# Batched 8 KB casting loads, interleaved transposes, two-bank evacuations and one store queue in a Q·Kᵀ kernel

## Chip, cores and metric

The kernel runs on one core of a Trainium2 chip. The metric is the device time of one execution in microseconds (us). Most figures are medians of several executions. In every run that lists both, the time is about 1.8 us above the span of the profile (for example 1071.39 and 1069.6 us for one execution of the changed kernel).

## The reference

```python
batch, n_heads, seq, head_dim = 8, 12, 1024, 64      # q, k: float32, 96 heads
np.einsum('bhid,bhjd->bhij', q, k).astype(np.float32)  # out: 8 x 12 x 1024 x 1024 float32
```

The kernel reads 50.3 MB and writes 402.7 MB. The product itself is small, so this is a kernel about moving bytes.

## The kernel before

For each head, two DMAs on the GpSimd queue load Q and K and cast them from float32 to float16. Partition p gets rows 8p to 8p+7 of the head. That is one run of 2 KB in memory, written as 1 KB. PE transposes both (K twice, for the upper and the lower 64 partitions), DVE copies the transposes to SBUF, PE makes 16 products of 128x512, and DVE and ACT evacuate each PSUM bank. (PE writes its products to PSUM; a bank here is a tile of 128x512 float32, and to evacuate it is to copy it to SBUF, from where it is stored.) One store of 4 MB per head goes out, on the SP queue for even heads and on the ACT queue for odd ones.

```python
    in_pool = ctx.enter_context(tc.tile_pool(name="in_pool", bufs=24))
    out_pool = ctx.enter_context(tc.tile_pool(name="out_pool", bufs=5))
    ...
    for bh in range(BH):
        q_sb = in_pool.tile([P, NT, D], MM_DT, tag="in")
        k_sb = in_pool.tile([P, NT, D], MM_DT, tag="in")
        nc.gpsimd.dma_start(out=q_sb, in_=qf[bh].rearrange("(p t) d -> p t d", p=P))
        nc.gpsimd.dma_start(out=k_sb, in_=kf[bh].rearrange("(p t) d -> p t d", p=P))
        ...  # 4 transposes of Q, 16 of K; 2 copies by DVE
        for n in range(2):
            for t in range(NT):
                ps = po_pool.tile([P, 512], mybir.dt.float32, tag="po")
                nc.tensor.matmul(ps, ...)
                ...  # evacuated by DVE or ACT, one bank at a time
        out_eng = nc.sync if bh % 2 == 0 else nc.scalar
        out_eng.dma_start(out=of[bh].rearrange("(p t) j -> p (t j)", p=P), in_=o_sb)
```

Of the kernel before, what the change touches and what calls it, by code (L numbers as in the profile page):

```python
# [1 line left out]

# [5 lines left out]


MM_DT = mybir.dt.float16


@with_exitstack
def kernel(
    ctx: ExitStack,
    tc: tile.TileContext,
    q: bass.AP,
    k: bass.AP,
    out: bass.AP,  # L20
):
    nc = tc.nc

    B, H, S, D = q.shape
    P = 128
    NT = S // P
    assert D == 64 and S % P == 0 and NT == 8

    qf = q.rearrange("b h s d -> (b h) s d")
    kf = k.rearrange("b h s d -> (b h) s d")  # L30
    of = out.rearrange("b h i j -> (b h) i (j)")
    BH = B * H

    consts = ctx.enter_context(tc.tile_pool(name="consts", bufs=1))
    ident = consts.tile([P, P], MM_DT)
    make_identity(nc, ident)

    in_pool = ctx.enter_context(tc.tile_pool(name="in_pool", bufs=24))
    tr_pool = ctx.enter_context(tc.tile_pool(name="tr_pool", bufs=3))
    out_pool = ctx.enter_context(tc.tile_pool(name="out_pool", bufs=5))  # L40
    pt_pool = ctx.enter_context(tc.tile_pool(name="pt_pool", bufs=1, space=bass.MemoryType.PSUM))
    po_pool = ctx.enter_context(tc.tile_pool(name="po_pool", bufs=6, space=bass.MemoryType.PSUM))

    for bh in range(BH):
        q_sb = in_pool.tile([P, NT, D], MM_DT, tag="in")
        k_sb = in_pool.tile([P, NT, D], MM_DT, tag="in")
        nc.gpsimd.dma_start(out=q_sb, in_=qf[bh].rearrange("(p t) d -> p t d", p=P))  # L47
        nc.gpsimd.dma_start(out=k_sb, in_=kf[bh].rearrange("(p t) d -> p t d", p=P))  # L48

        t_ps = pt_pool.tile([P, 12, P], MM_DT, tag="pt")  # L50
        qT_ps = t_ps[:, 0:4]
        kT_ps = t_ps[:, 4:12]
        for e in range(4):
            nc.tensor.transpose(qT_ps[:, e], q_sb[:, 2 * e : 2 * e + 2], ident)  # L54
        for t in range(NT):
            nc.tensor.transpose(kT_ps[0:64, t], k_sb[:, t], ident)  # L56
            nc.tensor.transpose(kT_ps[64:128, t], k_sb[:, t], ident)  # L57

        qT_sb = tr_pool.tile([P, 4, P], MM_DT, tag="qT")
        kT_sb = tr_pool.tile([P, P, NT], MM_DT, tag="kT")  # L60
        nc.vector.tensor_copy(out=qT_sb, in_=qT_ps)  # L61
        nc.vector.tensor_copy(out=kT_sb, in_=kT_ps.transpose([0, 2, 1]))  # L62
        kT_j = kT_sb.rearrange("pp p t -> pp (p t)")

        o_sb = out_pool.tile([P, NT, S], mybir.dt.float32, tag="out")
        for n in range(2):
            for t in range(NT):
                h = (t % 2) * 64
                e = t // 2
                ps = po_pool.tile([P, 512], mybir.dt.float32, tag="po")  # L70
                nc.tensor.matmul(  # L71
                    ps,
                    qT_sb[h : h + 64, e],
                    kT_j[h : h + 64, n * 512 : (n + 1) * 512],
                )
                idx = n * NT + t
                if idx % 2 == 0 and idx < 14:
                    nc.vector.tensor_copy(  # L78
                        out=o_sb[:, t, n * 512 : (n + 1) * 512], in_=ps
                    )  # L80
                else:
                    nc.scalar.copy(  # L82
                        out=o_sb[:, t, n * 512 : (n + 1) * 512], in_=ps
                    )
        out_eng = nc.sync if bh % 2 == 0 else nc.scalar
        out_eng.dma_start(
            out=of[bh].rearrange("(p t) j -> p (t j)", p=P), in_=o_sb
        )


# [1 line left out]
_INS = ['q', 'k']  # L92
_OUTS = [((8, 12, 1024, 1024), 'float32')]


# [23 lines left out]
```

## Time and profile before

The time is 1075.96 us, the median of three executions (1073.93 to 1078.4). The profile has a span of 1077.5 us.

| | before |
|---|---|
| PE, DVE, ACT busy | 61%, 52%, 44% of the span |
| DMA engines | busy from start to end |
| a store packet (32 KB) | 1213 ns on ACT's queue, 1226 ns on SP's (medians of the packet records) |
| a load packet (2 KB read, 1 KB written) | 98 ns (median) |

The lines below are the DMA rows of the page's 40 slices and its queue table. In the queue table, q1 and q10 are the store queues of SP and ACT, q0 is the casting loads and q8 fetches PE's instructions. The last column is the time of the packets as a share of 16 engines' span.

```profile
DMA  9999999999999999999999999999999999999998
GB/s 230 391 426 420 428 415 386 422 355 421 422 385 392 422 425 360 421 423 397 367 422 426 347 421 423 386 396 364 421 417 391 393 422 421 353 419 423 353 425 373
...
q1 hardware_dynamic: 6912, 201.33, 43.8%
q10 hardware_dynamic: 6912, 201.33, 43.6%
q0 software_dynamic: 27648, 25.18, 14.5%
q8 instruction: 27, 0.44, 0.1%
```

Every digit of the DMA row is 9 but the last, so the engines are the limit. The GB/s row counts written bytes. A cast writes half of what it reads, so a slice full of loads looks slow in that row without being slow. Most dips to about 350 are such slices. The last one also holds a real gap: from 1012 to 1016 us the DMA share is 0.24.

From the view of waits (engine, line, what it waited for: us in total, times, longest):

```profile
PEld L56 <- DMA k_sb<-in_k_dram: 210.4, 31, 16.9
PE t_ps L56 <- DMA k_sb<-in_k_dram: 192.7, 23, 16.0
PE t_ps L54 <- DMA q_sb<-in_q_dram: 114.2, 15, 14.1
DVE o_sb L78 <- DMA out_dram<-o_sb: 7.1, 3, 3.6
ACT o_sb L82 <- DMA out_dram<-o_sb: 6.5, 3, 2.8
```

PE waits for loads. It hardly ever happens that an output buffer is still full. From the issue table, a load of 128 KB takes 34.7 to 39.5 us to land:

```profile
q_sb<-in_q_dram POOLq DMA_DIRECT2D x96, 128.0 KB, 39.5
k_sb<-in_k_dram POOLq DMA_DIRECT2D x96, 128.0 KB, 34.7
```

### The profile page before, as it was taken

Reading aid. Unit: us, or ns where it says so; the run is one execution under the profiler, and the core shown is the slowest. Engines: PE = TensorE matmul, PEld = TensorE weight load, DVE = VectorE, ACT = ScalarE, POOL = GpSimd, SP = SyncE. Lnnn points to the kernel's source line nnn. Section 1 sums busy time; section 2 is a strip of 40 time slices with the busy share of each in tenths; the row PEclk is TensorE's granted clock in tenths of the full one; section 3 lists DMA queues with packets and bytes.
Section 4 is the critical chain, followed back from the end, with each engine's and each line's share of the span. In section 5 each row is a group of like instructions: output and inputs, shape, how many; then the busy total and the mean of one; then the engine's idle time right before and its main releaser. Section 6 shows DMA issues by size and latency. Waiting matters only on the chain.

```text
span 1077.5 us, 9569 instructions
## 1 busy us (share of the span) xinstructions
PE 654.1 (61%) x3456; PEld 211.4 (20%) x3456; DVE 564.9 (52%) x864; ACT 469.5 (44%) x865; POOL 102.1 (9%) x198
## 2 busy tenths in 40 slices
PE   6888428458718627817693784665871862684470
PEld 2222102112202202202221221111220220221120
DVE  5686426447618625816473482544761862483360
ACT  4475315336506514615362462434650651463360
POOL 6100001020002002000200200102000100200000
PEclk9995555656556755855555565555655675565555
DMA  9999999999999999999999999999999999999998
GB/s 230 391 426 420 428 415 386 422 355 421 422 385 392 422 425 360 421 423 397 367 422 426 347 421 423 386 396 364 421 417 391 393 422 421 353 419 423 353 425 373
DMA packets 41519, 428.44 MB, mean 398 GB/s; under 512 B 4608, under 2 KB 29184, under 8 KB 29184
## 3 DMA queue, kind: packets, MB, share of 16 engines
q1 hardware_dynamic: 6912, 201.33, 43.8%
q10 hardware_dynamic: 6912, 201.33, 43.6%
q0 software_dynamic: 27648, 25.18, 14.5%
q8 instruction: 27, 0.44, 0.1%
q14 instruction: 20, 0.16, 0.0%
HBM read 50.33 MB, written 402.65 MB: 420 GB/s over the span
## 4 chain that ended last, share of the span: by engine, by line
PE 34%; another core or an unknown queue 25%; DMA 21%; DVE 15%; issue 2%; ACT 1%; POOL 0%; DVEq 0%; POOLq 0%; ACTq 0%
PE ps L71 21%; DMA q_sb<-in_q_dram 13%; DVE o_sb L78 7%; DVE kT_sb L62 6%; PE t_ps L56 5%; DMA k_sb<-in_k_dram 5%; PE t_ps L57 4%; PE t_ps L54 4%; DMA out_dram<-o_sb 3%; DVE qT_sb L61 1%; ACT o_sb L82 1%; POOL q_sb L47 0%; POOL k_sb L48 0%; DVEq L78 0%
## 5 line engine op out<-in xcount | busy, mean ns | idle before, releaser
L82 ACT COPY o_sb<-ps 128x512 f32<-128x512 f32 x864 | 468.2, 595 | 577.4 <-PE ps L71 564.9
L78 DVE COPY o_sb<-ps 128x512 f32<-128x512 f32 x672 | 427.3, 682 | 212.3 <-ACT o_sb L82 124.4
L71 PE MATMUL ps<-kT_sb,qT_sb 64*128 64x512 f16 x1536 | 485.7, 552 | 39.0 <-DVE o_sb L78 29.6
L56 PE MATMUL t_ps<-ident,k_sb 128*64 128x128 f16 x768 | 143.1, 303 | 192.7 <-DMA k_sb<-in_k_dram 192.7
L61 DVE COPY qT_sb<-t_ps 128x512 f16<-128x512 f16 x96 | 40.2, 418 | 269.4 <-PE ps L71 258.6
L54 PE MATMUL t_ps<-ident,q_sb 128*128 128x128 f16 x384 | 68.5, 280 | 160.5 <-DMA q_sb<-in_q_dram 114.2
L57 PE MATMUL t_ps<-ident,k_sb 128*64 128x128 f16 x768 | 151.5, 303 | 0.0
L71 PEld LDWEIGHTS <-qT_sb 64*128 64x128 f16 x1536 | 94.5, 105 | 195.1 <-issue 162.2
L56 PEld LDWEIGHTS <-k_sb 128*64 128x64 f16 x768 | 74.0, 144 | 250.6 <-DMA k_sb<-in_k_dram 210.4
L62 DVE COPY kT_sb<-t_ps 128x1024 f16<-128x1024 f16 x96 | 116.4, 1213 | 0.0
L57 PEld LDWEIGHTS <-k_sb 128*64 128x64 f16 x768 | 76.9, 143 | 107.7 <-issue 107.7
L47 POOL DMA_DIRECT2D q_sb<-in_q_dram x96 | 51.1, 532 | 423.9 <-PE ps L71 146.8
L48 POOL DMA_DIRECT2D k_sb<-in_k_dram x96 | 50.9, 530 | 423.7 <-PE t_ps L57 205.3
L54 PEld LDWEIGHTS <-q_sb 128*128 128x128 f16 x384 | 31.6, 113 | 280.7 <-issue 145.9
L82 ACT ACT_TABLE_LOAD x1 | 1.3, 1283 | 0.7 <-PEq L103 0.7
masks.py:199 POOL TENSOR_SCALAR_AFFINE_SELECT ident<-ident 128x128 f16<-128x128 f16 x1 | 0.3, 305 | 0.1
masks.py:197 POOL MEMSET ident<- 128x128 f16 x1 | 0.2, 204 | 0.3 <-POOLq L103 0.3
L103 POOL MEMSET const-float32-0.0<- 128x1 f32 x1 | 0.1, 98 | 0.2 <-issue 0.2
L103 POOL MEMSET const-bfloat16-1.0<- 128x1 bf16 x1 | 0.1, 101 | 0.0
L103 POOL MEMSET const-uint8-127<- 128x1 uint8 x1 | 0.1, 101 | 0.0
L103 POOL MEMSET const-float32-1.0<- 128x1 f32 x1 | 0.1, 98 | 0.0
## 6 DMA issues: line engine op xcount, KB each, us to landing
out_dram<-o_sb SPq DMA_DIRECT2D x48, 4096.0 KB, 25.6
out_dram<-o_sb ACTq DMA_DIRECT2D x48, 4096.0 KB, 26.8
q_sb<-in_q_dram POOLq DMA_DIRECT2D x96, 128.0 KB, 39.5
k_sb<-in_k_dram POOLq DMA_DIRECT2D x96, 128.0 KB, 34.7
```

The costliest lines, as they stand in the source:

```text
L47: nc.gpsimd.dma_start(out=q_sb, in_=qf[bh].rearrange("(p t) d -> p t d", p=P))
L48: nc.gpsimd.dma_start(out=k_sb, in_=kf[bh].rearrange("(p t) d -> p t d", p=P))
L54: nc.tensor.transpose(qT_ps[:, e], q_sb[:, 2 * e : 2 * e + 2], ident)
L56: nc.tensor.transpose(kT_ps[0:64, t], k_sb[:, t], ident)
L57: nc.tensor.transpose(kT_ps[64:128, t], k_sb[:, t], ident)
L61: nc.vector.tensor_copy(out=qT_sb, in_=qT_ps)
L62: nc.vector.tensor_copy(out=kT_sb, in_=kT_ps.transpose([0, 2, 1]))
L71: nc.tensor.matmul(ps, qT_sb[h : h + 64, e], kT_j[h : h + 64, n * 512 : (n + 1) * 512],)
L78: nc.vector.tensor_copy(out=o_sb[:, t, n * 512 : (n + 1) * 512], in_=ps)
L82: nc.scalar.copy(out=o_sb[:, t, n * 512 : (n + 1) * 512], in_=ps)
L103: nc = _bacc.Bacc("TRN2", target_bir_lowering=False, num_devices=1)
```

## The change

The intent is to make loads cheaper and earlier. Q and K of four heads are loaded by one DMA each, so that a partition gets a run of 8 KB. The next batch's transposes are placed between this batch's products, evacuations take two banks at once, and all stores go to the SP queue, which leaves ACT free.

Because partition p now holds 32 rows of a four-head block, DVE has to spread the transposed rows over the heads. It uses four small strided copies for Q instead of one.

The core of the diff:

```diff
-    in_pool = ... bufs=24          # one head each
-    out_pool = ... bufs=5
-    po_pool = ... bufs=6           # tiles of one bank
+    sizes = [1, 1, 2] + [GMAX] * (BH // GMAX - 1)     # GMAX = 4
+    in_pool = ... bufs=4           # a batch of up to four heads each
+    out_pool = ... bufs=4
+    po_pool = ... bufs=3           # tiles of two banks
...
+            for src, dst in ((qf, self.q_sb), (kf, self.k_sb)):
+                nc.gpsimd.dma_start(
+                    out=dst[:, : self.R],
+                    in_=src[rows].rearrange("(p r) d -> p r d", p=P),
+                )
...
+            for g in range(G):
+                ms = slice(g * pp, (g + 1) * pp)
+                nc.vector.tensor_copy(out=qT[:, g, :, :, a], in_=t_ps[:, 0:4, ms])
+            nc.vector.tensor_copy(out=kT[:, :, :, a], in_=t_ps[:, 4:12].rearrange("c t (g m) -> c g m t", g=G))
...
+                ps = po_pool.tile([P, S], F32, tag="po")
+                for n in range(2):
+                    nc.tensor.matmul(ps[:, n * 512 : (n + 1) * 512], ...)
+                if t in (1, 4, 6):
+                    nc.vector.tensor_copy(out=o_sb[:, t], in_=ps)
+                else:
+                    nc.scalar.copy(out=o_sb[:, t], in_=ps)
-        out_eng = nc.sync if bh % 2 == 0 else nc.scalar
-        out_eng.dma_start(...)
+            nc.sync.dma_start(...)
...
+    for i, b in enumerate(batches):
+        if i + AHEAD < len(batches):          # AHEAD = 3
+            batches[i + AHEAD].load()
+        for g in range(b.G):
+            b.scores(g)
+            ... nxt.transpose(a)              # the next batch's transposes
```

More of the change, by code (lines that the diff above doesn't have):

```diff
@@ L8 @@
 from concourse._compat import with_exitstack
-MM_DT = mybir.dt.float16
+F16 = mybir.dt.float16
+F32 = mybir.dt.float32
+P = 128
 @with_exitstack
@@ L24 @@
     B, H, S, D = q.shape
-    P = 128
     NT = S // P
-    assert D == 64 and S % P == 0 and NT == 8
-    qf = q.rearrange("b h s d -> (b h) s d")
-    kf = k.rearrange("b h s d -> (b h) s d")
-    of = out.rearrange("b h i j -> (b h) i (j)")
     BH = B * H
-    consts = ctx.enter_context(tc.tile_pool(name="consts", bufs=1))
-    ident = consts.tile([P, P], MM_DT)
-    make_identity(nc, ident)
-    in_pool = ctx.enter_context(tc.tile_pool(name="in_pool", bufs=24))
-    tr_pool = ctx.enter_context(tc.tile_pool(name="tr_pool", bufs=3))
@@ L40 @@
-    out_pool = ctx.enter_context(tc.tile_pool(name="out_pool", bufs=5))
-    pt_pool = ctx.enter_context(tc.tile_pool(name="pt_pool", bufs=1, space=bass.MemoryType.PSUM))
-    po_pool = ctx.enter_context(tc.tile_pool(name="po_pool", bufs=6, space=bass.MemoryType.PSUM))
-    for bh in range(BH):
-        q_sb = in_pool.tile([P, NT, D], MM_DT, tag="in")
-        k_sb = in_pool.tile([P, NT, D], MM_DT, tag="in")
-        nc.gpsimd.dma_start(out=q_sb, in_=qf[bh].rearrange("(p t) d -> p t d", p=P))
-        nc.gpsimd.dma_start(out=k_sb, in_=kf[bh].rearrange("(p t) d -> p t d", p=P))
-        t_ps = pt_pool.tile([P, 12, P], MM_DT, tag="pt")
-        qT_ps = t_ps[:, 0:4]
-        kT_ps = t_ps[:, 4:12]
-        for e in range(4):
-            nc.tensor.transpose(qT_ps[:, e], q_sb[:, 2 * e : 2 * e + 2], ident)
-        for t in range(NT):
-            nc.tensor.transpose(kT_ps[0:64, t], k_sb[:, t], ident)
-            nc.tensor.transpose(kT_ps[64:128, t], k_sb[:, t], ident)
-        qT_sb = tr_pool.tile([P, 4, P], MM_DT, tag="qT")
-        kT_sb = tr_pool.tile([P, P, NT], MM_DT, tag="kT")
-        nc.vector.tensor_copy(out=qT_sb, in_=qT_ps)
-        nc.vector.tensor_copy(out=kT_sb, in_=kT_ps.transpose([0, 2, 1]))
-        kT_j = kT_sb.rearrange("pp p t -> pp (p t)")
-        o_sb = out_pool.tile([P, NT, S], mybir.dt.float32, tag="out")
-        for n in range(2):
@@ new lines @@
+    GMAX = 4
+    assert D == 64 and NT == 8 and BH % GMAX == 0
+    qf = q.rearrange("b h s d -> (b h s) d")
+    kf = k.rearrange("b h s d -> (b h s) d")
+    of = out.rearrange("b h i j -> (b h) i j")
+    sizes = [1, 1, 2] + [GMAX] * (BH // GMAX - 1)
+    assert sum(sizes) == BH
+    consts = ctx.enter_context(tc.tile_pool(name="consts", bufs=1))
+    ident = consts.tile([P, P], F16)
+    in_pool = ctx.enter_context(tc.tile_pool(name="in_pool", bufs=4))
+    tr_pool = ctx.enter_context(tc.tile_pool(name="tr_pool", bufs=2))
@@ new lines, with __init__, load, alloc @@
+    out_pool = ctx.enter_context(tc.tile_pool(name="out_pool", bufs=4))
+    pt_pool = ctx.enter_context(
+        tc.tile_pool(name="pt_pool", bufs=1, space=bass.MemoryType.PSUM)
+    )
+    po_pool = ctx.enter_context(
+        tc.tile_pool(name="po_pool", bufs=3, space=bass.MemoryType.PSUM)
+    )
+    class Batch:
+        def __init__(self, first, G):
+            self.first, self.G, self.R = first, G, 8 * G
+        def load(self):
+            rows = slice(self.first * S, (self.first + self.G) * S)
+            self.q_sb = in_pool.tile([P, GMAX * NT, D], F16, tag="q")
+            self.k_sb = in_pool.tile([P, GMAX * NT, D], F16, tag="k")
+            for src, dst in ((qf, self.q_sb), (kf, self.k_sb)):
+                nc.gpsimd.dma_start(
+                    out=dst[:, : self.R],
+                    in_=src[rows].rearrange("(p r) d -> p r d", p=P),
+                )
+        def alloc(self):
+            self.qT = tr_pool.tile([P, GMAX * 4 * P], F16, tag="qT")
+            self.kT = tr_pool.tile([P, GMAX * S], F16, tag="kT")
+        def transpose(self, a):
+            G, pp = self.G, P // self.G
+            t_ps = pt_pool.tile([P, 12, P], F16, tag="pt")
+            for e in range(4):
+                r = a * NT + 2 * e
+                nc.tensor.transpose(t_ps[:, e], self.q_sb[:, r : r + 2], ident)
+            for t in range(NT):
+                rows = self.k_sb[:, a * NT + t]
+                nc.tensor.transpose(t_ps[0:64, 4 + t], rows, ident)
+                nc.tensor.transpose(t_ps[64:128, 4 + t], rows, ident)
+            qT = self.qT[:, : G * 4 * P].rearrange(
+                "c (g e m a) -> c g e m a", g=G, e=4, m=pp
+            )
+            kT = self.kT[:, : G * S].rearrange(
+                "c (g m a t) -> c g m a t", g=G, m=pp, t=NT
+            )
+            for g in range(G):
+                ms = slice(g * pp, (g + 1) * pp)
+                nc.vector.tensor_copy(out=qT[:, g, :, :, a], in_=t_ps[:, 0:4, ms])
+            nc.vector.tensor_copy(
+                out=kT[:, :, :, a],
+                in_=t_ps[:, 4:12].rearrange("c t (g m) -> c g m t", g=G),
+            )
+        def scores(self, g):
+            bh = self.first + g
+            qT = self.qT.rearrange("c (g e m) -> c g e m", e=4, m=P)
+            kT = self.kT.rearrange("c (g j) -> c g j", j=S)
+            o_sb = out_pool.tile([P, NT, S], F32, tag="out")
@@ L67 @@
             for t in range(NT):
                 h = (t % 2) * 64
-                e = t // 2
-                ps = po_pool.tile([P, 512], mybir.dt.float32, tag="po")
-                nc.tensor.matmul(
-                    ps,
-                    qT_sb[h : h + 64, e],
-                    kT_j[h : h + 64, n * 512 : (n + 1) * 512],
-                )
-                idx = n * NT + t
-                if idx % 2 == 0 and idx < 14:
-                    nc.vector.tensor_copy(
-                        out=o_sb[:, t, n * 512 : (n + 1) * 512], in_=ps
-                    )
-                else:
-                    nc.scalar.copy(
-                        out=o_sb[:, t, n * 512 : (n + 1) * 512], in_=ps
-                    )
@@ L85 @@
-        out_eng = nc.sync if bh % 2 == 0 else nc.scalar
-        out_eng.dma_start(
-            out=of[bh].rearrange("(p t) j -> p (t j)", p=P), in_=o_sb
-        )
+                ps = po_pool.tile([P, S], F32, tag="po")
+                for n in range(2):
+                    nc.tensor.matmul(
+                        ps[:, n * 512 : (n + 1) * 512],
+                        qT[h : h + 64, g, t // 2],
+                        kT[h : h + 64, g, n * 512 : (n + 1) * 512],
+                    )
@@ new lines, in scores @@
+                if t in (1, 4, 6):
+                    nc.vector.tensor_copy(out=o_sb[:, t], in_=ps)
+                else:
+                    nc.scalar.copy(out=o_sb[:, t], in_=ps)
+            nc.sync.dma_start(
+                out=of[bh].rearrange("(p t) j -> p (t j)", p=P),
+                in_=o_sb.rearrange("p t j -> p (t j)"),
+            )
+    batches, first = [], 0
+    for G in sizes:
+        batches.append(Batch(first, G))
+        first += G
+    AHEAD = 3
+    for b in batches[:AHEAD]:
+        b.load()
@@ new lines @@
+    make_identity(nc, ident)
+    batches[0].alloc()
+    for a in range(batches[0].G):
+        batches[0].transpose(a)
+    for i, b in enumerate(batches):
+        if i + AHEAD < len(batches):
+            batches[i + AHEAD].load()
+        nxt = batches[i + 1] if i + 1 < len(batches) else None
+        if nxt:
+            nxt.alloc()
+        for g in range(b.G):
+            b.scores(g)
+            if nxt:
+                for a in range(g * nxt.G // b.G, (g + 1) * nxt.G // b.G):
+                    nxt.transpose(a)
```

## The prediction

> **What bounds the kernel now.** The DMA engines, by bytes. The page's slices show them 90% busy or more from start to end; its queue table gives the store queues 43.8% + 43.6% and the load queue 14.5% of 16 engines' span, together 102% (packet records overlap a little). PE is busy 61%, DVE 52%, ACT 44%. A late stretch without loads (1040 to 1060 us) moves 423 to 432 GB/s. The Trainium skill ("DMA: Bandwidth & Descriptors", Where 436 GB/s comes from) puts the ceiling at 435 GB/s; this trace agrees within some 1 to 3%.
>
> In the packet records a store packet (32 KB) takes 1213 ns; a load packet (2 KB read, 1 KB written) 98 ns. In the pure-load stretch (9 to 18 us) the loads write 200 GB/s, so read 400 GB/s: about 82 ns a packet net of overlap, against 75 ns for 2 KB at the stores' rate. The 50.3 MB of reads already run at over 90% of line rate; that is why I expect little.
>
> Estimate from these numbers: 402.7 MB at 431 GB/s is 934 us; 24576 load packets at 82 ns on 16 engines, 126 us; 7 us of start and end; sum 1067. The other 10 us of the 1077.5 us span are holes and overhead. At 1011 to 1016 us the stores have run dry and PE waits 11 us for q_sb; some 3.7 us of DMA time is lost. Near 744 to 750 us about 1.2 us more.
>
> **Why the holes.** The queues take turns packet by packet (the skill, same page, Queues, rings and completion order). The trace agrees: from 60 to 140 us, loads read 0.26 MB per 20 us, one 2 KB packet for two 32 KB store packets. Loads starve (q_sb lands 39.5 us after issue) until the stores run dry. PE waits 307 us for q_sb and k_sb (waits view), mostly while DMA is busy.
>
> **What the change does.**
> - 8 KB load packets, a quarter as many: estimated 301 ns plus 8 to 20 fixed, in place of 4 x 82. Saves about 6 us (3 to 8).
> - One store queue, 8 KB per turn: loads get 1/5 of the bytes and need 1/9. Late holes close: about 5 us.
> - Two-bank evacuations, interleaved transposes, four strided qT copies in place of one: per head I estimate ACT 5 x 1.05 us, DVE 3 x 1.25 plus 2, PE 7. A store takes 9.7 us, with loads 11. All off the path.
> - One store queue for two: nothing; stretches with one or two move 430 to 432 GB/s alike.
> - Start: loads go out 0.7 us earlier, the identity 3 us later (after seven issues of 0.55 us); a wash. 4 output buffers suffice.
>
> Gain: about 11 us of DMA time, plus 2 to 3 us of smaller gaps.
>
> **Predicted: 1062 us, range 1055 to 1069. Faster by over 2%: 0.08; within 2%: 0.90; slower by over 2%: 0.02.**
>
> **What would show it.** Load packets 27648 to about 7500; share 14.5% to about 11.5%; stores still about 87%; no late dip. PE's waits on q_sb and k_sb shrink from 307 us to under 50; ACT and DVE wait for out_dram<-o_sb (13.6 us before) for hundreds of us: compute blocked by full output buffers. The chain becomes mostly stores.
>
> **What would make it wrong.** Faster than 1055: two store queues cost switching time that I don't see, or loads hide behind stores. Slower than 1069: an 8 KB cast packet costs over 330 ns; strided DVE copies, or PE stalled on the single transpose buffer, push compute beyond 11 us a head; an uneven share among the engines leaves tails.

## More of the kernel before

The kernels of one call ran on one chip together with the kernel before.

## The result

The changed kernel takes 1071.83 us (median of four executions, 1071.3 to 1072.35), against 1076.89 us for the kernel before beside it (four executions). The ratio is 0.9955, with a 95% interval of 0.9938 to 0.9972. Ratios here are the mean time of one kernel's runs over that of the other's of the same rounds, so they are not quite the ratio of the medians.

In e10 the changed kernel took 1070.61 us (ratio 0.9925, interval 0.9901 to 0.9949). The gain is about 5 to 7 us. 14 us had been predicted, and the time lies above the predicted range.

The same lines of the profile after (q0 are the loads, q1 all stores; there is no q10):

```profile
DMA  9999999999999999999999999999999999999996
GB/s 213 394 382 386 380 400 414 394 420 396 410 410 384 422 398 410 411 389 419 401 397 424 390 419 401 400 419 389 415 406 399 422 430 430 429 434 432 431 431 292
...
q1 hardware_dynamic: 13824, 402.66, 88.0%
q0 software_dynamic: 7488, 25.17, 11.9%
q8 instruction: 27, 0.44, 0.1%
```

The late dips are gone, and after the last load (837 us) the stores run at 422 to 434 GB/s. But the very last slice is down to 6 tenths and 292 GB/s. The waits:

```profile
ACT o_sb L114 <- DMA out_dram<-o_sb: 359.1, 87, 7.3
DVE o_sb L112 <- DMA out_dram<-o_sb: 213.8, 47, 7.5
PEld L78 <- DMA q_sb<-in_q_dram: 4.2, 1, 4.2
```

The mechanism turned round as it was meant to. PE waits 4.2 us for loads (before a weight load), and 573 us of ACT's and DVE's idle time is waiting for a free output buffer. From the chain that ended last, by engine, first before and then after:

```profile
PE 34%; another core or an unknown queue 25%; DMA 21%; DVE 15%; issue 2%; ACT 1%; POOL 0%; DVEq 0%; POOLq 0%; ACTq 0%
DMA 77%; PE 7%; ACT 7%; DVE 1%; issue 0%; ACTq 0%
```

So what is the last slice? The next lines give stretches of the end of both profiles. The columns are the stretch and its length in us, the busy time of each engine, PE's granted clock, the mean share of the 16 DMA engines that is busy, and GB/s. First the kernel before:

```profile
1060.00:1070.00 10.00, 0.00 (x0) 0.00 (x0) 0.00 (x0) 0.00 (x0) 0.00 (x0) 0.50 1.07 459
1070.00:1074.00 4.00, 0.00 (x0) 0.00 (x0) 0.00 (x0) 0.00 (x0) 0.00 (x0) 0.50 0.95 410
1074.00:1077.00 3.00, 0.00 (x0) 0.00 (x0) 0.00 (x0) 0.00 (x0) 0.00 (x0) 0.50 0.03 11
```

And the changed kernel:

```profile
1040.00:1050.00 10.00, 0.00 (x0) 0.00 (x0) 0.00 (x0) 0.00 (x0) 0.00 (x0) 0.50 1.02 439
1050.00:1058.00 8.00, 0.00 (x0) 0.00 (x0) 0.00 (x0) 0.00 (x0) 0.00 (x0) 0.50 0.98 422
1058.00:1062.00 4.00, 0.00 (x0) 0.00 (x0) 0.00 (x0) 0.00 (x0) 0.00 (x0) 0.50 0.57 246
1062.00:1066.00 4.00, 0.00 (x0) 0.00 (x0) 0.00 (x0) 0.00 (x0) 0.00 (x0) 0.50 0.19 82
1066.00:1069.00 3.00, 0.00 (x0) 0.00 (x0) 0.00 (x0) 0.00 (x0) 0.00 (x0) 0.50 0.03 11
```

In the kernel before, the DMA engines stop together. In the changed one they stop one after the other over 10 us: a share of 0.19 is three of sixteen engines. No compute engine has anything left to do.

A store raises its semaphore once for each of the 16 engines that finish their part of it, so the trace has 16 landing times for each store. They show how far apart the engines are. For the last store (my count from the semaphore records; us from the span's start):

| kernel | first | mean of 16 | second last | last | time (median) |
|---|---|---|---|---|---|
| before | 1074.9 | 1075.1 | 1075.6 | 1076.6 | 1076.9 |
| changed | 1058.4 | 1062.0 | 1067.0 | 1068.7 | 1071.8 |

The average engine gained 13.1 us, and the last one 7.9 us. The profile of e10, the changed kernel again, has the same tail: mean 1061.6, last 1067.9. In the changed kernel the distance between the first and the last landing (here called the lag) grows through the run:

```
store number     0    16    32    48    64    80    95
before          3.4   2.6   2.6   1.7   0.9   4.8   1.7   us
changed         1.4   4.7   6.1   7.2   7.6   8.6  10.3   us
```

### The profile page after: what moved, and what is told of

Its sections match the earlier page's. It is cut to its first block, busy times and chain, and to the rows that moved or that the text cites. A ratio compares the mean times of both kernels' runs of the same rounds, so it can differ in the third digit from the quotient of the medians.

```text
span 1069.6 us, 8844 instructions
## 1 busy us (share of the span) xinstructions
PE 627.9 (59%) x3456; PEld 214.0 (20%) x3456; DVE 565.7 (53%) x758; ACT 468.4 (44%) x481; POOL 28.2 (3%) x58
## 3 DMA queue, kind: packets, MB, share of 16 engines
q0 software_dynamic: 7488, 25.17, 11.9%
## 4 chain that ended last, share of the span: by engine, by line
DMA 77%; PE 7%; ACT 7%; DVE 1%; issue 0%; ACTq 0%
DMA out_dram<-o_sb 77%; ACT o_sb L114 7%; PE ps L106 6%; DVE kT L92 0%; DVE qT L91 0%; PE t_ps L81 0%; PE t_ps L78 0%; DVE o_sb L112 0%; PE t_ps L82 0%; ACTq L114 0%
## 5 line engine op out<-in xcount | busy, mean ns | idle before, releaser
L114 ACT COPY o_sb<-ps 128x1024 f32<-128x1024 f32 x480 | 467.1, 1014 | 566.5 <-DMA out_dram<-o_sb 359.1
L106 PE MATMUL ps<-kT,qT 64*128 64x512 f16 x1536 | 480.9, 597 | 270.8 <-ACT o_sb L114 227.2
L112 DVE COPY o_sb<-ps 128x1024 f32<-128x1024 f32 x288 | 351.7, 1223 | 374.0 <-DMA out_dram<-o_sb 213.8
L106 PEld LDWEIGHTS <-qT 64*128 64x128 f16 x1536 | 101.0, 109 | 605.2 <-issue 580.0
L91 DVE COPY qT<-t_ps 128x128 f16<-128x128 f16 (+1 forms) x374 | 121.2, 469 | 95.7 <-PE t_ps L82 95.7
L78 PE MATMUL t_ps<-ident,q_sb 128*128 128x128 f16 x384 | 56.4, 299 | 135.9 <-DVE kT L92 130.2
L92 DVE COPY kT<-t_ps 128x1024 f16<-128x1024 f16 x96 | 118.8, 1237 | 0.0
L81 PE MATMUL t_ps<-ident,k_sb 128*64 128x128 f16 x768 | 102.5, 310 | 0.0
L82 PE MATMUL t_ps<-ident,k_sb 128*64 128x128 f16 x768 | 102.4, 310 | 0.0
L64 POOL DMA_DIRECT2D q_sb<-in_q_dram x26 | 14.0, 537 | 767.5 <-PE t_ps L78 766.8
L64 POOL DMA_DIRECT2D k_sb<-in_k_dram x26 | 13.9, 534 | 13.2 <-PE t_ps L82 13.2
```

The source lines that it names most:

```text
L64: nc.gpsimd.dma_start(out=dst[:, : self.R], in_=src[rows].rearrange("(p r) d -> p r d", p=P),)
L78: nc.tensor.transpose(t_ps[:, e], self.q_sb[:, r : r + 2], ident)
L81: nc.tensor.transpose(t_ps[0:64, 4 + t], rows, ident)
L82: nc.tensor.transpose(t_ps[64:128, 4 + t], rows, ident)
L91: nc.vector.tensor_copy(out=qT[:, g, :, :, a], in_=t_ps[:, 0:4, ms])
L92: nc.vector.tensor_copy(out=kT[:, :, :, a], in_=t_ps[:, 4:12].rearrange("c t (g m) -> c g m t", g=G),)
```

## Experiments

The theory after the result had two parts. First, the changed kernel never lets the stores run dry, so the slowest DMA engine sets the time and the average engine no longer matters. Second, something slows some engines. Candidates were the software queue of the casting loads, the instruction fetches, and the loads themselves. All edits are to the changed kernel. The sections say where an experiment failed.

### e1: two store queues again

```diff
-            nc.sync.dma_start(
+            (nc.sync if bh % 2 == 0 else nc.scalar).dma_start(
```

> The changed kernel, with its stores alternating between the SP and ACT queues again. If one store queue in place of two is what the change gained or lost by, this run moves back to the time before (1077 us) or down to the 1062 us that was predicted. My theory is that the number of store queues matters little: 1070 to 1075 us; loads get a smaller turn (one packet in three), but 8 KB packets still give them 1/9 of the bytes, just what they need. The lag of the slowest DMA engine at the last store (10.3 us between first and last landing in the changed kernel) stays at 6 to 12 us.

Measured: 1073.51 us (ratio 0.9951, interval 0.9921 to 0.998), so the store queues account for little or nothing. The landings of the last store lie 3.1 us apart, not 6 to 12; that expectation failed. It failed in an instructive way. The engines end closer together here (mean 1068.9, last 1071.2 us), 7 us of tail have become 2, and still the time is no better: the mean landing comes 7 us later instead. Two stretches of e1:

```profile
840.00:880.00 40.00, 23.38 (x132) 8.11 (x130) 21.34 (x30) 15.55 (x17) 0.00 (x0) 0.50 0.95 404
1068.00:1071.00 3.00, 0.00 (x0) 0.00 (x0) 0.00 (x0) 0.00 (x0) 0.00 (x0) 0.50 0.13 55
```

And the same early stretch of the changed kernel:

```profile
840.00:880.00 40.00, 25.75 (x142) 8.68 (x141) 23.48 (x32) 19.46 (x20) 0.00 (x0) 0.50 1.00 431
```

So lining the engines up did not by itself bring time. Where the 7 us went is shown only in part. In this stretch a share of 0.05 of 40 us, 2 us, is idle. In three others (from 260, 620 and 720 us) the share is the same in both kernels, 1.01 to 1.02, while e1 moves 397, 394 and 396 GB/s and the changed kernel 410, 403 and 402. In e1 the evacuations also wait more for PE (ACT 451.8 us, against 207.0) and less for free buffers (241 us, against 573). e1 therefore agrees with the theory that the slowest engine sets the time, but does not prove it; e6, which was to test it, failed.

### e2: loads of one head, 2 KB runs

```diff
-    GMAX = 4
+    GMAX = 1
-    sizes = [1, 1, 2] + [GMAX] * (BH // GMAX - 1)
+    sizes = [1] * BH
-    in_pool bufs=4, AHEAD = 3
+    in_pool bufs=16, AHEAD = 12
```

> The changed kernel with batches of one head (2 KB runs, 192 loads), twelve heads ahead as before. Theory: the 2 KB packets cost about 6 us of DMA time more per engine, and starve again beside the stores, so the store queue runs dry now and then as in the kernel before: 1075 to 1082 us, load share of the DMA time 14.5% again, and the lag of the slowest engine at the last store small again (under 5 us), because every time the stores run dry the engines line up. Rival (the gain came from the interleaving and the two-bank evacuations): 1070 to 1074 us.

Measured: 1077.32 us, ratio 0.9992 (0.9956 to 1.0027). The load share is 14.3%, the landings of the last store lie 1.9 us apart, and PE waits for K again (198.3 us). So without the 8 KB runs (and the batches that go with them) nothing of the gain is left: the interleaving, the two-bank evacuations and the single store queue alone give nothing that can be measured. What the 8 KB runs would give without the rest was not run.

### e3: no software queue

```diff
-                nc.gpsimd.dma_start(out=dst[:, : self.R], in_=...)
+                raw = raw_pool.tile([P, GMAX * NT, D], F32, tag=tag)
+                nc.scalar.dma_start(out=raw[:, : self.R], in_=...)
+                nc.gpsimd.tensor_copy(out=dst[:, : self.R], in_=raw[:, : self.R])
```

> The changed kernel with the loads moved off the GpSimd queue: fp32 loads of the same 8 KB runs on the ACT queue, cast on GpSimd by a copy. Rival A (the software queue of the casting loads slows some DMA engines, which makes the lag of 10 us): the last store's landings lie within 4 us of each other and the time falls to 1062 to 1066 us. Rival B (instruction fetches and other traffic on some engines make the lag): the lag stays at 7 to 12 us, and the time at 1069 to 1074 us.

Measured: 1087.25 us. The start is slower (with one raw buffer the first loads wait for each other), and that says nothing about the question. The tail does. The last landing comes at 1083.9 us and the one before it at 1077.7, so the tail is longer than with the software queue. Rival A, that the software queue makes the lag, falls. The lag of 16.8 us is also above the 7 to 12 of rival B, and the time is outside both forecasts.

### e4 and e5: more and fewer PE instructions

```diff
+                for _ in range(2):                       # e4: each transpose issued twice
                     nc.tensor.transpose(...)
```
```diff
                 nc.tensor.transpose(t_ps[0:64, 4 + t], rows, ident)
-                nc.tensor.transpose(t_ps[64:128, 4 + t], rows, ident)     # e5
+            nc.vector.tensor_copy(out=kT[0:64, :, :, a], in_=kT_in)       # both from t_ps[0:64]
+            nc.scalar.copy(out=kT[64:128, :, :, a], in_=kT_in)
```

> The changed kernel with every transpose issued twice into the same place: 20 more weight load and matmul pairs a head, 55% more PE instructions, so 42 instead of 27 fetches of 16 KB; PE still under 11 us a head. Rival B (instruction fetches make the lag): the lag of the slowest engine at the last store grows from 10.3 us to 13 us or more and the time by 2 to 5 us. Rival A (the software queue): lag and time unchanged within 1.5 us.

> The changed kernel with each K row transposed once instead of twice; the copy for partitions 64 to 127 is made by ACT from the same PSUM half. 28 instead of 36 weight load and matmul pairs a head, so 21 instead of 27 fetches of 16 KB. From the run with 42 fetches (lag 14.2 us against 10.3, time about 4.8 us more, so some 0.3 us a fetch) the theory that instruction fetches make the lag expects a lag of 8 to 9.5 us at the last store and 1069 to 1071 us. If the fetches had nothing to do with it (the run before was slow for its extra PE work), no change within 1 us.

Measured: e4 takes 1076.66 us with 42 fetches of 16 KB. The landings are 14.2 us apart, the mean landing is 1063.6 and the last 1073.6 us. e5 takes 1068.26 us with 21 fetches (ratio 0.9911, 0.9883 to 0.9939).

The time of e4 fits the theory of fetches. That of e5 fell too, a little below the 1069 to 1071 us expected. The lag of e5 does not fit: 12.9 us instead of 8 to 9.5. Its first landing came earlier (1055.2), its last (1068.2) hardly; but the profile is of its slowest execution (1070.83 us).

### e6: two output buffers

```diff
-    out_pool = ... bufs=4
+    out_pool = ... bufs=2
```

> The changed kernel with 2 output buffers instead of 4, so that a fast DMA engine can be at most one store ahead of the slowest. Theory (the slowest engine is never idle, and its work is the bound; the tail is only where the others' spare time shows): the lag at the last store falls under 4 us, and still the time stays within 1070 to 1075 us, for the idle time of the other engines only moves from the end into the run. Rival (the tail is a cost of its own at the end, which a run with lined-up engines doesn't pay): 1062 to 1067 us. If filling a buffer (7 to 8 us) is too slow for two buffers, all engines have gaps and the time rises over 1080 us; then this run tells nothing of the two.

Measured: 1111.73 us. This is the case in which it tells nothing: the landings are 1.9 us apart, but two buffers are too few for all engines.

### e7: which engine is it?

```diff
+                for n in (8, 4, 12, 14, 15, 6, 10, 2, 48, 9):    # last head only
+                    nc.sync.dma_start(out=dst[at : at + n], in_=src[at : at + n])
```

> The changed kernel, with the last head stored in ten pieces of 8, 4, 12, 14, 15, 6, 10, 2, 48 and 9 partitions. By the Trainium skill (DMA: Bandwidth & Descriptors, how many engines) a piece of n partitions under 16 goes to the n lowest-numbered engines. The landings of each piece then tell which of the 16 lags belong to low-numbered engines. No theory says which engines lag; if it is the fetches of one queue, I expect the same few engines at each time. The time itself says nothing here: low engines get more of the last store.

Measured (one execution, state unknown): 1088.85 us. Each piece of n < 16 partitions raised its semaphore n times from DMAs, as the page says. The slowest engine lands the store before at 1066.6 us, and then finishes one piece after the other: those of 8, 12, 14, 15, 6 and 10 partitions last at 1068.7, 69.9, 73.6, 74.8, 76.0 and 77.2 us.

The piece of 4 was complete at 1062.6 us, before the slowest engine had even finished the store ahead of it. So the slowest engine takes part in a piece of 6 and not in one of 4 (no other landing of the piece of 6 is later than 1068.9). If engines are given out from the lowest number, it is the fifth or the sixth. Work can therefore not be taken from it alone by choosing the number of partitions, because by that numbering every engine above it would lose the same share.

### e8, e11 and e17: more instructions elsewhere

```diff
+            for _ in range(72):                     # e8; 48 in e11
+                nc.gpsimd.memset(junk, 0.0)
```
```diff
+            nc.gpsimd.tensor_copy(out=junk[0:1], in_=o_sb[0:1, NT - 1, S - 1 :])   # e17
+            for _ in range(39):
+                nc.gpsimd.memset(junk[0:1], 0.0)
```

> The changed kernel with 72 one-element fills a head on GpSimd into a tile that nobody reads: 6912 more instructions, 442 KB more to fetch, and no more work for PE, DVE, ACT or the stores. GpSimd stays under 8 us a head. Theory (instruction fetches take DMA time from the stores, whichever engine they are for): time up by 3 to 8 us to 1075 to 1080 us, the landings of the last store later on average. Rival (the run with doubled transposes was slow for its PE work): 1071 to 1073 us.

> Mend of the run with 72 fills a head, in which GpSimd fell behind with issuing the loads: 48 one-element fills a head on GpSimd (by that run about 0.16 us each, so 7.7 us of the 11 us of a head), 4608 more instructions, 36 more fetches of 8 KB, no more work for PE, DVE, ACT or the stores. Theory (instruction fetches take DMA time from the stores, for whichever engine): 1072.5 to 1077 us against 1070.6 to 1071.8 us for the changed kernel. Rival (the run with doubled transposes was slower for its PE work, not for its fetches): 1070 to 1072 us. If PE waits for q_sb or k_sb by more than 30 us, the loads were late again and the run tells nothing.

> The changed kernel with one one-element copy of o_sb and 39 one-element fills a head on GpSimd; the copy ties them to the head, so that they cannot run ahead of the loads as in the two failed runs. 3840 more instructions, 30 more fetches of 8 KB, no more work for PE, DVE, ACT or the stores. If fetches cost DMA time whoever needs them: up by 1.5 to 4 us, 1072 to 1076 us. If the doubled transposes cost time by PE's work and not by fetches: 1070 to 1072.5 us. If PE waits over 30 us for q_sb and k_sb: no verdict, as before.

Measured: e8 1361.42 us and e11 1202.61 us. Both failed. The fills depended on nothing, so they were ordered far ahead of the next loads on GpSimd (427 fills in one go between two loads in e11), and PE waited 394 and 193 us for Q. They say nothing about the question.

In e17 the copy ties the fills to their head, and PE no longer waits for loads. It takes 1078.32 us, 6 to 8 us more than the changed kernel (on other chips) and 11 us more than e18, and above both expectations. The mean landing did not move (1061.4 us, against 1062.0 and 1061.6). One engine alone lands at 1075.4 us, 19.1 us after the first and 4.9 us after the second last. Stretches of e17's end:

```profile
1056.00:1062.00 6.00, 0.00 (x0) 0.00 (x0) 0.00 (x0) 0.00 (x0) 0.00 (x0) 0.50 0.53 229
1062.00:1066.00 4.00, 0.00 (x0) 0.00 (x0) 0.00 (x0) 0.00 (x0) 0.00 (x0) 0.50 0.15 66
1066.00:1070.00 4.00, 0.00 (x0) 0.00 (x0) 0.00 (x0) 0.00 (x0) 0.00 (x0) 0.50 0.11 49
1070.00:1075.00 5.00, 0.00 (x0) 0.00 (x0) 0.00 (x0) 0.00 (x0) 0.00 (x0) 0.50 0.06 26
```

A share of 0.06 is one engine of sixteen. 3840 tiny instructions on an engine that was nearly idle cost about 7 us. It shows on the late engines: the last landing moved from 1068.7 to 1075.4 us, the second last from 1067.0 to 1070.5. That the mean did not move does not tell against the fetches: 30 packets of 309 ns on 16 engines would move it by 0.6 us (an estimate), hardly more than two profiles of the changed kernel differ. One side effect was not foreseen. The copy reads o_sb, so ACT and DVE waited 170.3 and 98.2 us for GpSimd before they filled a buffer again; up to 1056 us the DMA engines stay busy all the same.

### e9, e10 and e18: fewer instructions, and the changed kernel again

```diff
-            for t in range(NT):
-                rows = self.k_sb[:, a * NT + t]
-                nc.tensor.transpose(t_ps[0:64, 4 + t], rows, ident)
-                nc.tensor.transpose(t_ps[64:128, 4 + t], rows, ident)
+                nc.tensor.transpose(t_ps[:, 4 + e], self.k_sb[:, r : r + 2], ident)   # in the loop over e
-            nc.vector.tensor_copy(out=kT[:, :, :, a], in_=...)
+            for o in range(2):          # even rows lie in the lower half, odd rows in the upper
+                kT_in = t_ps[o * 64 : o * 64 + 64, 4:8].rearrange("c e m -> c m e")
+                nc.vector.tensor_copy(out=kT[0:64, :, a, :, o], in_=kT_in)
+                nc.scalar.copy(out=kT[64:128, :, a, :, o], in_=kT_in)
```

e9 and e18 are this version, with two smaller buffers for the transposes in place of one. e10 is the changed kernel itself.

> The changed kernel with K transposed in pairs of rows like Q (4 pairs of instructions a head instead of 16), and the halves copied to both partition halves, two copies on DVE and two on ACT: 24 instead of 36 weight load and matmul pairs a head, 18 instead of 27 fetches of 16 KB by PE. From 21 fetches (1068.3 us), 27 (1071.8) and 42 (1076.7), about 0.4 us a fetch, I expect 1066 to 1068.5 us, below both kernels. Without a cost of fetches: 1071 to 1073 us.

> The changed kernel itself, in the same call, as the measure for the other two and for how much the lag of the slowest engine at the last store differs between profiles of one kernel: 1071 to 1073 us, lag 8 to 13 us.

> The version with 24 matmul pairs a head again, on another chip: 1066 to 1070 us, ratio to the kernel before 0.988 to 0.993; if the first five rounds were luck, 1070 to 1073 us like the changed kernel.

Measured: e9 1068.28 us (1066.38 to 1071.73; ratio to the kernel before 0.9909, 0.9881 to 0.9936). e10 on the same chip 1070.61 us (1070.46 to 1071.13; 0.9925). e18 on another chip 1067.28 us (1066.28 to 1068.62; 0.9892, 0.9871 to 0.9914).

The version is the fastest by its medians, but hardly faster than e5 (1068.26 us). It is about 1% faster than the kernel before, and by the medians 2 us to 5 us faster than the changed kernel; the intervals overlap. e10 fell just below its 1071 to 1073 us, with a lag of 11.2 us. e9 alone would not have shown a gain over the changed kernel, since two of its six executions took 1071.6 us and more. Its last landings are 1066.1 (e9) and 1063.9 us (e18), its means 1061.4 and 1059.7.

Queue lines of e18, for comparison with the changed kernel: the same stores and loads, 18 fetches instead of 27.

```profile
q1 hardware_dynamic: 13824, 402.66, 88.2%
q0 software_dynamic: 7488, 25.17, 11.9%
q8 instruction: 18, 0.29, 0.1%
```

### e12 to e16: the lag by itself

```diff
+            if self.first > GMAX:       # e12, e16: later batches use the fourth batch's Q and K
+                self.q_sb, self.k_sb = batches[3].q_sb, batches[3].k_sb
+                return
```

e13 also skips the transposes and the qT and kT copies from the fifth batch on. e14 skips only the copies, e15 only the transposes. Their outputs are wrong, which doesn't matter for the times.

> The changed kernel with only the first eight heads loaded; all later batches compute from the fourth batch's Q and K, so the result is wrong on purpose. 27 fetches and all the stores stay, 92% of the load packets go. Theory A (the fetches alone make the lag of the slowest DMA engine): the last store's landings spread by 7 to 12 us as before. Theory B (loads beside stores make part of it): the spread falls to 3 to 6 us. Time 950 to 965 us either way.

> The run without later loads, and from the fifth batch on without transposes and qT, kT copies (wrong result on purpose). If the transposing phase slows one DMA engine, the spread of the last store's landings falls from 15.3 us to under 4 us. If that engine is slow by itself beside any saturated store, it stays above 10 us.

> The run without later loads, with all PE transposes but from the fifth batch on without the qT and kT copies of DVE (wrong on purpose). If PE's instructions (their number, fetches, reads of the identity) slow the engine: spread 10 to 16 us as without loads. If DVE's copies do: under 4 us.

> The run without later loads, with all qT and kT copies of DVE but from the fifth batch on no PE transposes, so half the PE instructions and 13 or 14 fetches instead of 27 (wrong on purpose). If DVE's copies slow the engine: spread 10 to 16 us. If PE's instructions do: under 4 us.

> The run without later loads again (wrong on purpose), on the same chip as the three others, as their measure: one engine about 15 us behind at the last store, the second under 5 us, if this is a property of the kernel; something else if it is a property of one chip or one execution.

Measured: 977.65 us for e12 (two executions; 950 to 965 had been expected), 963.12, 982.6, 964.32 and 977.59 us for e13 to e16 (one execution each, state unknown; mainly the landings are used). The lag is between the first landing and the last. Those of e12 to e15 all fell outside the ranges named beforehand:

| run | PE transposes | qT, kT copies | fetches of 16 KB | lag at last store | second last engine |
|---|---|---|---|---|---|
| e12 (chip 2) | yes | yes | 27 | 15.3 us | 2.9 us |
| e16 (chip 6) | yes | yes | 27 | 15.3 us | 2.9 us |
| e14 (chip 6) | yes | no | 27 | 6.7 us | 2.3 us |
| e15 (chip 6) | no | yes | 13 | 9.0 us | 2.3 us |
| e13 (chip 6) | no | no | 13 | 7.5 us | 2.2 us |

Without loads it is exactly one engine that lags. The end of e12:

```profile
958.00:962.00 4.00, 0.00 (x0) 0.00 (x0) 0.00 (x0) 0.00 (x0) 0.00 (x0) 0.50 0.59 254
962.00:966.00 4.00, 0.00 (x0) 0.00 (x0) 0.00 (x0) 0.00 (x0) 0.00 (x0) 0.50 0.08 33
966.00:970.00 4.00, 0.00 (x0) 0.00 (x0) 0.00 (x0) 0.00 (x0) 0.00 (x0) 0.50 0.06 25
970.00:975.00 5.00, 0.00 (x0) 0.00 (x0) 0.00 (x0) 0.00 (x0) 0.00 (x0) 0.50 0.05 20
```

Two chips give 15.29 and 15.30 us, so this belongs to the program and not to a chip or to chance. The engine loses time steadily (0.1 to 0.28 us a store against the middle engine, from about 200 us on), not in steps at the fetches. In e13 nothing is fetched between 654 and 732 us, and its last engine falls behind there as fast as elsewhere, from 5.1 to 5.5 us in six stores. So the packets of the fetches are not what slows this engine. In e12 the loss slows to about 0.12 us a store when the transposes end (877 us), and stops only when the evacuations end (942 us).

e14 cannot be read as it was meant. Nothing held its transposes back, and they were ordered ahead, as the fills of e8 and e11 were: the last one starts at 188 us, and 17 of the 27 fetches come by 191 us. In that time the stores ran dry. After it e14 is e13 over again. The rows of PE and DMA over the run, e12 first and then e14:

```profile
PE   6785868777666666766657667666666665766430
DMA  7999899999999999999999999999999999999993
PE   5799999894545454545454545454545454545430
DMA  8999887999999999999999999999999999999997
```

So transposes spread over the run, without the copies, were not tested. The copies alone add 1.5 us to e13 (e15), transposes and copies together 7.8. Theory B of e12, that loads are part of it, falls for this one engine: without loads the lag of the worst engine is larger, not smaller, though fewer engines lag.

One regularity covers these runs; it was found in the traces after all runs. In stretches without loads, one engine's time per store goes with the number of instructions that all compute engines together run per store (my count, weight loads included; stores 36 to 86 of e12 to e16, 76 to 86 of e3, e4 and e17, and the last two stores, after all compute, for none):

| instructions per store | last engine, us per store | middle engine |
|---|---|---|
| none (e12 to e16) | 9.67 to 9.68 | 9.69 to 9.71 |
| 40 (e13, e14) | 9.80 to 9.81 | 9.73 |
| 45 (e15) | 9.81 to 9.82 | 9.73 to 9.74 |
| 85 (e12, e16, e3) | 9.91 to 9.92 | 9.71 to 9.75 |
| 124 to 125 (e4, e17) | 10.01, 10.05 | 9.72 to 9.75 |

That is about 3 ns an instruction (an estimate from this table), alike for PE's (e4) and GpSimd's (e17). No run was built to test it, and every execution comes with a profile's span and clock, so it is open whether the instructions themselves or their recording cost that engine its time. It is not the whole tail either. Where loads run, other engines fall behind too: in e5 the last engine is 9.5 us behind the middle one at 884 us and gains or loses little afterwards. What slows those is left open.

## Why the prediction was wrong

- **DMA engines as the limit, loads already at over 90% of line rate, little to gain: right.** The result is within 2%.
- **8 KB packets: right.** A packet of 8 KB takes 322 ns in the records (predicted 309 to 321; that was net of overlap, which the record is not, and the fixed part of 8 to 20 ns in it was not derived). There are 7488 packets (about 7500), and the share is 11.9% (11.5%).
- **Starving loads and late holes: right.** PE's waits for loads fell from 307 to 4.2 us of PE time ("under 50"). The waits for output buffers grew from 13.6 to 573 us ("hundreds"). The chain is 77% stores. e2 shows that no gain is left without the long runs.
- **Compute off the path: right.** ACT took 1014 ns for an evacuation (predicted 1.05 us), DVE 1223 ns (1.25 us).
- **One store queue for two changes nothing in the time: right** (e1), though the engines end closer together with two.
- **The predicted time: wrong.** The step that failed is the sum. It divided the work evenly by 16 engines, and it listed "an uneven share among the engines leaves tails" only as a risk, with no time of its own. The sum was right for the average engine of the two profiled executions: its last landing moved from 1075.1 to 1062.0 us, 13.1 us, where "about 11 us of DMA time, plus 2 to 3 us of smaller gaps" had been predicted. But the distance from the mean to the last landing grew from 1.5 us (1076.6 - 1075.1) to 6.7 us (1068.7 - 1062.0). Of the 13.1 us, 5.2 were given back there.
- **The remaining 2 to 3 us** are the base. The profile before fell on a slower execution (span 1077.5, so about 1079.3 us by the offset of 1.8 us, an estimate) than the median of 1076.9 us. So some 2.4 of the average engine's 13.1 us are luck of that execution, and the sum was a little too high there as well. For one execution of the changed kernel the account closes: 1062.0 (mean landing) + 6.7 (to the last) + 0.9 (to the end of the span, 1069.6) + 1.8 (to the time) = 1071.4 us.

The trace before held a warning that I did not read. In the kernel before, one engine was 4.1 to 4.4 us late for three of the stores from number 91 to 94, while the second last was 1.8 to 2.0 us late. In the kernel before, whose queues ran dry now and then, the lag was 1.7 us again at the last store; in the changed one, which kept them full, it added up.

## What to carry to other kernels

A kernel that keeps all DMA engines busy to the end is finished when the slowest engine is. Look at the 16 landings of a store over the run, and at the last slice, not only at the mean busy share. Closing holes in the DMA time can bring less than their size if slow engines used them to catch up. Loads that compete with stores want long runs; how much of that is their turn at the engines and how much their own cost, no run here separates. Instructions on idle engines were not free here: tiny ones cost about 7 us (e17), and the two versions with fewer PE instructions had the lowest medians (e5, e9 with e18). When an experiment leaves out an instruction, look in the trace whether the rest still runs at the same time: in e8, e11 and e14 it did not.

## What the Trainium skill lacked or had wrong

- "DMA: Bandwidth & Descriptors" says of engines 7 and 15 that they are usually slower, with the software queue's descriptor rings as a best guess. Here the slowest engine took part in a piece of 6 partitions and not in one of 4 (e7), so by the page's own numbering it is not 7 or 15. The lag was larger without the software queue (e3: 16.8 us between first and last landing, against 10.3) and with hardly any loads (e12: 15.3 us).
- The same page does not tell that one engine can fall behind steadily under stores without a pause: 15.3 us in 960, the same on two chips. Nor does it tie a DMA engine's time to what the compute engines run: here 9.67 us a store with no instructions, 9.91 with 85.
- The same page does not say which side of a casting load counts for its bandwidth. Here it is the read side: loads that write 200 GB/s read 400 GB/s, near the page's 435 GB/s.
- The same page gives the number of engines that a small piece uses, which e7 confirms, but not what many of them in one queue do to a packet. In the last 40 us of e7 some 32 KB packets took 3 to 9.3 us instead of 1.21.
- "Runtime: NRT & Kernel Launch", Instruction fetch mechanics, gives blocks of 16 KiB (256 instructions) for each engine. The trace agrees for PE (27 packets of 16 KB for 6912 instructions), but the packets of the other fetch queue, q14, are 8 KB. It also calls the cost of a block boundary mostly hidden. No run here tells against that: more or fewer instructions (e4, e17, e18) moved the time by up to 7 us, but in e13 the last engine fell behind alike where nothing was fetched.
